# Conformer convolution on eight cores: convolution in four pieces between the next chunk's projections, last chunk in two token halves, normalised block and y written over spent u

## The chip, the cores and the metric

The kernel runs on the eight cores of one Trainium2 chip, two sequences per core and no traffic between the cores. The time is the device time of the slowest core, in microseconds (us). Executions fall into two states. In the slow state one die (cores 0 to 3 or 4 to 7) runs long at a lowered clock and the time is longer. All times here are of fast executions unless said otherwise.

Also in a "fast" execution a pair of neighbouring cores can run at clock 0.81. The clock record of the trace gives it as 0.8125, 13/16. I call such a pair *hit*.

## The reference, cut to what matters

The model has two layers (the first a gated linear recurrence, the second the convolution), each between SwiGLU feed-forward parts and followed by cross-attention. Only the convolution part changes. Per core it occurs twice, once for each sequence, at about 2040 to 2340 us and at about 4835 to 5135 us. I call these the two stages. T is 2048 tokens, D is 1024 channels (8 chunks of 128).

```python
def conformer_conv_mixer(h, w_in, b_in, dw, dw_b, ln_g, ln_b, w_out, b_out):
    a, gate = jnp.split(h @ w_in + b_in, 2, axis=-1)
    u = a * jax.nn.sigmoid(gate)                         # GLU, (B,S,D)
    u = lax.conv_general_dilated(u, dw..., padding=[(CONV_WIDTH - 1, 0)],
                                 feature_group_count=D) + dw_b     # depthwise, 31 taps, causal
    u = jax.nn.silu(layer_norm(u, ln_g, ln_b))           # LayerNorm over all 1024 channels
    return u @ w_out + b_out
```

The LayerNorm needs sums over all channels, so no token can be normalised before the convolution of its last channel chunk is done.

## The kernel before

A kernel-side list scheduler orders the instructions. The program adds operations with their reads, writes, assumed duration `d` and, for TensorE, the PSUM bank. The scheduler simulates the engines with these durations and fixes one instruction order per engine at build time.

The scheduler divides PSUM into eight banks (`NBANK = 8`). One chunk's convolution holds banks 0 to 3, the LayerNorm sums `bs` and `bq` hold two, and two are left for the projections while a convolution is held.

```python
def glu(c):                                   # projections of chunk c, 4 blocks of 512 tokens
    for blk in range(NB):
        bg = P.bank(); ba = P.bank()
        ...  # 2 x 8 matmuls 128x512 (line 948), sigmoid on ScalarE (L951),
        ...  # (a + b) * gate on VectorE (L952), 32x32 transposes into uP (L954)

def conv(c):                                  # depthwise convolution of chunk c
    b = P.bank(n=4)
    for hf in range(2):
        expand(...)                           # VectorE copies the taps into 128x128 form (L929)
        for jj in range(16):
            j = hf * 16 + jj
            for w in range(2):                # L973: N = 64 columns, read 32 elements (64 bytes) apart
                P.op("pe", ... rhs=up.ap[:, (1 - w) * 32 + j : ... : 32], ..., d=62)
    ...  # transposes out of PSUM into u2 (VectorE, L981/L987)
    ...  # per 512 tokens: copy and square (ScalarE, L991/L992), two sum matmuls (L994)

do_glu(0)
for c in range(1, KC):
    do_glu(c)
    if c - 1 < NW:                            # NW = 5
        conv(c - 1)
for c in range(min(NW, KC - 1), KC):
    conv(c)                                   # chunks 5, 6, 7: after all projections
...  # LayerNorm: mean, variance, Ln, Exp for all tokens (L1015-L1019)

def outp(blk):                                # one block of 512 tokens
    ...                                       # mean and rstd to 128 rows (L1027), rstd copied (L1028)
    for c in range(KC):
        n = nrm[c % 3]                        # three shared f32 buffers
        ...  # n = u2 + bias - mean (VectorE, L1032); n *= rstd (POOL, L1034)
        ...  # y = silu(n) (ScalarE, L1035)
    ...  # 64 output matmuls (L1042), sums added to h
```

The softmax here doesn't subtract the row's maximum and nothing guards it: scores larger than these inputs give would overflow.

## Time and profile before

| | before |
|---|---|
| time, median of fast runs | about 5739 us (5738.61, 5739.36, 5740.08; a slow run took 6629.12) |
| TensorE busy | 97% |
| first stage, core 1: first projection to first output matmul | 216.0 us |
| output part, first to last output matmul's end | 81.1 us |
| mean granted clock of an unhit core | 0.978 |

The list of cores gives the span and the mean granted clock of each. Cores 4 and 5 were hit in this execution (they ended 35 us later; their clock is 0.81 from about 3006 to 3166 us, in the second sequence's first part, which the change does not touch), the others not:

```profile
core 1: 5738.2 us, clock 0.977
core 4: 5771.1 us, clock 0.971
```

TensorE's timeline of core 4 in the steady part. The columns are start, duration, engine, line, operation, tiles, shapes and count. A bracket gives the idle time before and what ended it:

```profile
2074.91 7.24 PE L973 MATMUL ps<-arena 128*128 128x64 bf16 x64
2081.98 5.94 PE L948 MATMUL ps<-arena 128*128 128x512 bf16 x16
2087.85 0.60 PE L994 MATMUL ps<-arena,ones 128*32 128x512 bf16 x2
2088.39 1.90 PE L948 MATMUL ps<-arena 128*128 128x512 bf16 x8
```

Sixty-four convolution matmuls take 7.24 us, 113 ns each (about 110 without the tail of the last one, in the steady period). The 16 projections behind them take 5.94 us, where eight take 1.90 us a little later. The stretches of one microsecond show why (columns: window, length, TensorE busy and instructions, granted clock, share of DMA, GB/s):

```profile
2079.00:2080.00 1.00, 1.00 (x12) 0.93 1.07 217
2080.00:2081.00 1.00, 1.00 (x12) 0.50 0.96 193
2087.00:2088.00 1.00, 1.00 (x6) 1.00 0.17 29
```

The clock falls to 0.50 inside the convolution burst although TensorE is busy all the time, and is back at 1.00 at 2086.7 us, 4.7 us after the projections have resumed. The tail of the stage, same columns as the timeline above:

```profile
2211.85 7.24 PE L973 MATMUL ps<-arena 128*128 128x64 bf16 x64 [1.07 <-DVE arena L952]
...
2246.50 4.87 PE L994 MATMUL ps<-arena,ones 128*32 128x512 bf16 x8 [2.23 <-ACT arena L991]
...
2260.34 1.87 PE L1042 MATMUL ps<-arena 128*128 128x512 bf16 x4 [3.47 <-ACT arena L1035]
```

The last sum ends at 2251.4 us, the first output matmul starts at 2260.3 us. From 2216 to 2264 us the granted clock is 0.50.

### The profile page before, as it was taken

The page shows a single profiled execution, that of the slowest core. Times are in us where ns is not written, and L with a number is a line of the kernel's source. Part 1 is how long each engine was busy: PE and PEld are TensorE (multiplying, and loading weights), DVE is VectorE, ACT ScalarE, POOL GpSimd, SP SyncE. Part 2 cuts the span into 40 slices and gives each one's busy share as a digit, 9 for nine tenths or more (in the row PEclk, how much of TensorE's full clock was granted, in tenths as well). Part 3 has the DMA queues.
Part 4 walks back from the last instruction along what each step waited for, and adds up shares of the span by engine and source line. Part 5 has one row for each costly group of instructions (what it writes and reads, how often), then busy time and mean ns, then how long its engine had stood idle before and what let it go on. Part 6 is the DMA issues. An engine that isn't in the chain of part 4 may idle for free.

```text
span 5771.1 us, 89461 instructions; the slowest of 8 cores (5730.3 to 5771.1 us)
## 1 busy us (share of the span) xinstructions
PE 5594.7 (97%) x29808; PEld 2713.5 (47%) x29808; DVE 3522.3 (61%) x5299; ACT 1808.7 (31%) x2862; POOL 977.7 (17%) x1373
## 2 busy tenths in 40 slices
PE   7999999999999998999979999999999999989998
PEld 3444565444444454444434446644444444544443
DVE  5445767555765665555565566666656566565656
ACT  3323777311211134511130128762112112263112
POOL 2000444100100043200020014431001002241001
PEclk9999999999999998999988999999999999889999
DMA  6554122222222022121251212112222220221221
GB/s 148 108 106 103 30 37 45 42 37 41 37 37 41 15 41 55 34 48 34 45 146 33 35 32 33 32 38 55 35 43 37 41 37 8 48 59 23 37 41 63
DMA packets 84217, 283.14 MB, mean 49 GB/s; under 512 B 9408, under 2 KB 9408, under 8 KB 81216
## 3 DMA queue, kind: packets, MB, share of 16 engines
q0 software_dynamic: 59328, 197.16, 20.3%
q1 hardware_dynamic: 24448, 80.26, 4.1%
q8 instruction: 257, 4.21, 0.3%
q14 instruction: 184, 1.51, 0.1%
HBM read 440.96 MB, written 33.55 MB: 82 GB/s over the span
## 4 chain that ended last, share of the span: by engine, by line
PE 92%; DVE 2%; issue 2%; POOL 1%; ACT 1%; DMA 0%; DVEq 0%; SPq 0%; POOLq 0%; ACTq 0%
PE ps L638 42%; PE ps L654 21%; PE ps L1089 5%; PE ps L948 4%; PE ps L834 4%; PE ps L812 4%; PE ps L973 2%; PE ps L546 2%; PE ps L1161 2%; PE ps L1101 1%; PE ps L1042 1%; PE ps L732 1%; DVE hn_tok L542 1%; PE ps L994 1%; DVE h L658 1%
## 5 line engine op out<-in xcount | busy, mean ns | idle before, releaser
L638 PE MATMUL ps<-arena 128*128 128x512 bf16 x11264 | 2525.9, 382 | 4.1 <-DVE arena L552 3.1
L658 DVE SCALAR_TENSOR_TENSOR h<-ps,h 128x512 f32<-128x512 f32 x2816 | 1732.6, 681 | 41.0 <-PE ps L654 33.5
L638 PEld LDWEIGHTS ps<-arena 128*128 128x128 bf16 x11264 | 1106.7, 98 | 1345.1 <-issue 79.6
L641 DVE TENSOR_TENSOR arena<-ps,arena 128x512 bf16<-128x512 f32 x704 | 486.0, 691 | 1462.6 <-PE ps L638 1426.4
L640 ACT ACTIVATE arena<-ps 128x512 bf16<-128x512 f32 x704 | 420.3, 597 | 2842.6 <-PE ps L638 2832.5
L654 PE MATMUL ps<-arena 128*128 128x512 bf16 x5632 | 1301.4, 381 | 6.2 <-DVE arena L641 3.2
L654 PEld LDWEIGHTS ps<-arena 128*128 128x128 bf16 x5632 | 547.4, 98 | 682.0 <-issue 67.6
L574 POOL DMA_DIRECT2D arena<-ffn_w_in x176 | 96.0, 545 | 1834.4 <-PE ps L638 1651.9
L517 ACT ACTIVATE junk<-h 128x1024 bf16<-128x1024 f32 x288 | 303.5, 1054 | 263.3 <-DVE h L577 148.8
L542 DVE SCALAR_TENSOR_TENSOR hn_tok<-h,stat,gB 128x1024 bf16<-128x1024 f32 x256 | 332.8, 1307 | 64.8 <-POOL stat L521 25.9
L1089 PE MATMUL ps<-arena 128*128 128x512 bf16 x1536 | 363.0, 384 | 3.5 <-DVE arena L1123 2.6
L577 DVE TENSOR_TENSOR h<-ps,h 128x512 f32<-128x512 f32 x320 | 214.7, 686 | 112.4 <-PE ps L834 57.2
L520 POOL TENSOR_SCALAR stat<-stat 128x1 f32<-128x1 f32 x290 | 87.6, 302 | 995.9 <-ACT junk L517 980.7
L546 PE MATMUL ps<-ident,hn_tok 128*128 128x128 bf16 x2048 | 159.3, 228 | 95.7 <-DVE hn_tok L542 67.1
L948 PE MATMUL ps<-arena 128*128 128x512 bf16 x1024 | 246.4, 399 | 0.0
L521 POOL TENSOR_TENSOR stat<-stat,mhalf 128x1 f32<-128x1 f32 x290 | 232.9, 803 | 43.3 <-POOL stat L520 7.8
L812 PE MATMUL ps<-arena 128*128 128x512 bf16 x1024 | 234.9, 382 | 2.3 <-DVE arena L1134 2.3
L834 PE MATMUL ps<-arena 128*128 128x512 bf16 x1024 | 228.2, 379 | 0.0
L1089 PEld LDWEIGHTS ps<-arena 128*128 128x128 bf16 x1536 | 145.6, 99 | 159.5 <-issue 11.7
L546 PEld LDWEIGHTS ps<-ident,hn_tok 128*128 128x128 bf16 x2048 | 136.7, 102 | 148.8 <-issue 111.2
L574 POOL DMA_DIRECT2D arena<-ffn_w_out x88 | 48.0, 546 | 906.8 <-PE ps L654 905.8
L550 ACT ACTIVATE arena<-ps 128x1024 bf16<-128x1024 bf16 x128 | 130.5, 1021 | 132.8 <-PE ps L546 132.5
(121 smaller groups left out, 4097.9 us busy)
## 6 DMA issues: line engine op xcount, KB each, us to landing
arena<-ffn_w_in POOLq DMA_DIRECT2D x176, 512.0 KB, 6.8
arena<-ffn_w_out POOLq DMA_DIRECT2D x88, 512.0 KB, 6.2
h<-x SPq DMA_DIRECT2D x32, 512.0 KB, 7.3
arena<-hgrn_w_in POOLq DMA_DIRECT2D x64, 256.0 KB, 5.5
y<-arena SPq DMA_DIRECT2D x32, 512.0 KB, 3.3
arena<-xattn_wkv POOLq DMA_DIRECT2D x8, 1024.0 KB, 8.6
xattn_m<-arena SPq DMA_DIRECT2D x32, 256.0 KB, 3.1
xattn_v<-arena SPq DMA_DIRECT2D x16, 512.0 KB, 2.9
```

The lines of the kernel that those rows point to most:

```text
L517: P.op("act", lambda e: e.activation(out=junk[:], in_=src_tile_ap, func=AF.Square, accum_out=stat[:, 0, col:col + 1]), reads=rkeys, writes ...
L542: P.op("dve", lambda e, tt=tt, s=s: e.scalar_tensor_tensor(out=hn_tok[:, s, :], in0=h[:, tt, :], scalar=stat[:, 2, tt:tt + 1], in1=gB[:, g ...
L546: P.op("pe", lambda e, c=c, s=s, b=b: e.transpose(out=psb16(b)[:, c * 128:(c + 1) * 128], in_=hn_tok[:, s, c * 128:(c + 1) * 128], identit ...
L638: P.op("pe", lambda e, bb=bb, ga=ga, k=k, j=j: e.matmul(psb(bb), lhsT=wiv[:, ga, k, j * 128:(j + 1) * 128], rhs=hnT[:, k, blk * 512:(blk + ...
L640: P.op("act", lambda e, bg=bg, j=j: e.activation(out=sg[j].ap, in_=psb(bg), func=AF.Silu), reads=psk(bg), writes=sg[j].keys(), tbl=SILU)
L641: P.op("dve", lambda e, bu=bu, j=j: e.tensor_tensor(out=actv[:, j, :], in0=psb(bu), in1=sg[j].ap, op=ALU.mult), reads=psk(bu) + sg[j].keys ...
L654: P.op("pe", lambda e, bo=bo, j=j, t4=t4, half=half: e.matmul(psb(bo), lhsT=actv[:, j, t4 * 128:(t4 + 1) * 128], rhs=wov[:, j, half * 512: ...
L658: P.op("dve", lambda e, bo=bo, tt=tt, half=half: e.scalar_tensor_tensor(out=h[:, tt, half * 512:(half + 1) * 512], in0=psb(bo), scalar=0.5 ...
L812: P.op("pe", lambda e, b=b, k=k, mt=mt: e.matmul(psb(b), lhsT=mv[:, k, mt * 128:(mt + 1) * 128], rhs=hnT[:, k, blk * 512:(blk + 1) * 512], ...
L834: P.op("pe", lambda e, b=b, p=p, hh=hh, mt=mt, t4=t4, o=o: e.matmul(psb(b), lhsT=p.ap[:, mt * 512 + t4 * 128:mt * 512 + (t4 + 1) * 128], r ...
L948: P.op("pe", lambda e, bb=bb, a=a, k=k, blk=blk: e.matmul(psb(bb), lhsT=v[:, a, k, :], rhs=hnT[:, k, blk * 512:(blk + 1) * 512], start=(k ...
L1089: P.op("pe", lambda e, bb=bb, a=a, k=k: e.matmul(psb(bb), lhsT=v[:, a, k, :], rhs=hnT[:, k, blk * 512:(blk + 1) * 512], start=(k == 0), st ...
```

## The change

The intent has three parts.

1. *Interleave.* The convolution of chunk c-1 is cut into four pieces of 16 matmuls, one behind each block of 16 projections of chunk c, so that dense matmuls are never far apart.
2. *Halves.* The last chunk has no projections left to hide behind. It runs in two token halves (N = 32), each with its own sums and LayerNorm chain, so that the first half's chain overlaps the second half's convolution.
3. *In place.* u of seven chunks stays in SBUF, the normalisation works in place on u, and y is written over the u of the chunk before, which is spent. No shared buffers remain.

```diff
-            NW = 5
+            NH = 2 if NB >= 2 else 1
+            NW = KC - 1
...
-            nrm = [at(CP, 512, F32), at(CP + 2048, 512, F32), at(US, 512, F32)]
+            def ybuf(c, blk):
+                return y0[blk % 2] if c == 0 else at(u2[c - 1].off + blk * 2048, 512, BF16)
...
-            do_glu(0)
-            for c in range(1, KC):
-                do_glu(c)
-                if c - 1 < NW:
-                    conv(c - 1)
-            ...
+            for c in range(1, KC):
+                b = P.bank(n=4)
+                last = c == KC - 1
+                for blk in range(NB if not last else BH):
+                    glu(c, blk)
+                    for q in range(4 * blk // (BH if last else NB), 4 * (blk + 1) // (BH if last else NB)):
+                        piece(c - 1, q, b, 0, NBK)
+                out_of_psum(c - 1, b, 0, NBK)
+                for blk in range(NB):
+                    stats(c - 1, blk)
+            c = KC - 1
+            nb = NBK // NH
+            for hf in range(NH):
+                b = P.bank(n=2)
+                for q in range(4):
+                    if hf == 0 and NH > 1 and q < NB - BH:
+                        glu(c, BH + q)
+                    piece(c, q, b, hf * nb, nb)
+                out_of_psum(c, b, hf * nb, nb)
+                for blk in range(hf * BH, (hf + 1) * BH):
+                    stats(c, blk)
+                ln(hf)
...
                 for c in range(KC):
-                    n = nrm[c % 3]
-                    P.op("dve", ... out=pair(n.ap), in0=u2v(c, blk), ...)
+                    n = u2v(c, blk)
+                    y = ybuf(c, blk)
+                    P.op("dve", ... out=n, in0=n, ...)
```

The cuts ("...") leave out buffer addresses, the half-size `expand`, the split of the output weights into four loads, and the scheduler's two-bank allocation. Lines after the change: projection L975, sigmoid L978, multiply L979, transposes into uP L981, taps L955, convolution L998, transposes out of PSUM L1009/L1014, copy and square L1019/L1020, sums L1022, broadcasts L1080, rstd copy L1081, normalisation L1086 (VectorE) and L1088 (POOL), silu L1089, output L1098.

## The prediction

> **What bounds it now.** TensorE: page, PE 97% busy; chain of waits 92% PE. Only the two convolution stages change. TensorE's timeline: the first from 2044 us (first projection) to 2341 us, the second from 4874 us.
>
> First projection to first output-projection matmul (2260 us): 216 us. PE's work there, at the timeline's full-clock durations: 512 projections x 0.216 = 110.6, 512 conv matmuls x 0.1106 = 56.6, 64 sums x 0.27 = 17.3, transposes and LayerNorm broadcast 5: about 190 us. The 26 us excess:
>
> 1. Clock, steady chunks. Windows show the granted clock falling to 0.50 some 3 to 5 us after each 7.1 us conv burst begins, for 3.4 or 6.8 us. Conv matmuls keep 110 ns at either clock; the next 16 projections take 4.6 to 5.9 us, not 3.46: 7 us per stage. [...] drops at 2079.9, 2103.9, 2127.7 us lie multiples of 3.41 apart.
> 2. Clock, tail. From 2216 to 2264 us (conv of chunks 5 to 7, no projections left) it stays 0.50; sums take 0.58 instead of 0.27 us: 7 us.
> 3. PE's waits in the tail: sums, LayerNorm, first y: 11 us.
>
> **What the change does.**
> - Pieces of 16 conv matmuls (1.77 us) after 16 projections (3.46 us): every window holds at least 1.6 us of full-rate matmuls, so the clock should hold. A window with 0.7 us of projections (2148.1 to 2151.5) caused no drop; one with 0.3 did. Part 1 goes; conv of chunks 5 and 6 moves there, with most of part 2.
> - Chunk 7 stays bare, in halves of N=32. If the strided moving read (64 B apart) sets 110 ns, it halves: no extra PE work. If weight load, 7 us more per stage. I favour the read, since transposes load 128 columns every 56 ns[...].
> - The first half's LayerNorm chain (conv end to first output matmul: 16 us now) overlaps the second half's conv and sums, 6 to 9 us; 5 to 7 us stay idle.
> - y over spent u: output blocks prepare without three-buffer waits: 1 to 3 us. Block 0 stays paced at 1.23 us per chunk, later blocks by VectorE (18 us each).
> - Costs: conv and sums hold six banks, leaving two for projections; each has 3.5 to 5 us turnaround against 1 to 2 needed: 0 to 3 us. Expand copies halve in size, double in number.
>
> First output matmul comes near 198 us instead of 216 after the first projection: 18 us, plus 2 in the output part: 40 us over both stages, all on PE's path; 0.7%.
>
> **Prediction:** 5699 us, range 5680 to 5720. Faster by over 2%: 0.01; within 2%: 0.98; slower: 0.01.
>
> **Right if:** clock 1.0 from 2061 to about 2220 us; chunk period 23.1 us instead of 24.0 to 25.1; conv N=32 near 56 to 60 ns; first output matmul 16 to 20 us earlier; low clock only near chunk 7; mean clock about 0.985, not 0.978.
>
> **Wrong if:** two projection banks stall PE; N=32 conv stays at 110 ns (gain 26 us); interleaved windows still drop the clock; second LayerNorm and table loads delay block 0's silu; VectorE gives back the early start.

Two passages that did not come from this case's traces are cut from the recorded text. No term of its sum is among them: 18 us plus 2 per stage, 40 us over both stages, 5739 to 5699 us. A "window" in it is a step of 3.41 us: in the trace of the kernel before (core 4, clock record) every stretch of one clock between 2042 and 2285 us lasts 3.413 us or a multiple of it.

## More of the kernel before

Program order is priority. The order is part of the program, so an assumed duration that is wrong does not change it at run time (a convolution matmul is assumed at `d=62` ns and takes 110 in the trace).

One group of instructions, whole execution, core 4 (columns: count, busy time, mean ns of one, idle time before with its releasers):

```profile
L1032 DVE SCALAR_TENSOR_TENSOR arena<-arena,vecs,ps 128x512 f32<-128x512 f32 x64 | 46.7, 742 | 20.7 <-ACT arena L1035 9.8 <-POOL arena L1034 9.6 <-PE ps L1027 1.3
```

VectorE's subtraction of the mean waits 19.4 us for ScalarE and POOL to free one of the three shared buffers.

## The result, and the profile after

| | before | after |
|---|---|---|
| fast runs, us | 5738.61, 5739.36, 5740.08 | 5743.15, 5743.54, 5745.80 |
| ratio of fast runs | | 1.0008 (0.9986 to 1.0031): the same |
| unhit span, us (profiled execution) | about 5735 | about 5721 |
| mean clock, unhit core | 0.978 | 0.983 to 0.984 |
| pairs hit in these timed runs | none (the profiled execution: one) | 2, 2, 1 |
| first projection to first output matmul (first stage, cores 1 / 4) | 216.0 us | 216.8 us |
| output part (same cores) | 81.1 us | 64.9 us |

Ratios here and below are the mean time of one kernel's fast runs over that of the other's of the same rounds, so they are not quite the ratios of the medians that I quote. Predicted were 5699 us: the time stayed within 2%, as the prediction said, but the gain of 40 us did not come. Medians were 5744.67 us after (with its slow run of 5853.51) and 5739.72 us before.

Two things are hidden in "the same". First, the typical core did gain 14 us. Second, the slowest core hid it, as the list of cores after shows:

```profile
core 0: 5744.1 us, clock 0.979
core 1: 5743.9 us, clock 0.979
core 4: 5721.9 us, clock 0.984
```

Cores 0 and 1 ended 22 us later than the others with the same program. In TensorE's stretches they separate at one place: up to 2202 us core 0 has clock 1.00, after that 0.81 until about 2363 us (0.50 in the tail of the stage). First core 0, then core 4 (columns as before):

```profile
2195.60:2202.20 6.60, 6.60 (x32) 1.00 0.30 41
2203.00:2206.00 3.00, 3.00 (x13) 0.81 0.02 5
2270.00:2340.00 70.00, 70.00 (x315) 0.81 0.23 53
```

```profile
2203.00:2206.00 3.00, 3.00 (x18) 1.00 0.00 0
2270.00:2340.00 70.00, 68.30 (x403) 1.00 0.43 106
```

But an unhit core, too, is 22 us above the prediction, and its first output matmul comes no sooner. TensorE's timeline of core 4, an unhit one, shows what became of the interleave:

```profile
2109.00 1.93 PE L998 MATMUL ps<-arena 128*128 128x64 bf16 x16
2110.99 3.40 PE L975 MATMUL ps<-arena 128*128 128x512 bf16 x15
2114.32 0.61 PE L1022 MATMUL ps<-arena,ones 128*32 128x512 bf16 x2
2114.86 1.93 PE L998 MATMUL ps<-arena 128*128 128x64 bf16 x16
2116.71 0.60 PE L1022 MATMUL ps<-arena,ones 128*32 128x512 bf16 x2
2117.25 1.93 PE L998 MATMUL ps<-arena 128*128 128x64 bf16 x16
...
2119.64 1.93 PE L998 MATMUL ps<-arena 128*128 128x64 bf16 x16
2121.50 1.03 PE L1022 MATMUL ps<-arena,ones 128*32 128x512 bf16 x2
2122.87 11.23 PE L975 MATMUL ps<-arena 128*128 128x512 bf16 x47 [0.33 <-issue]
2133.94 1.93 PE L998 MATMUL ps<-arena 128*128 128x64 bf16 x16
```

The program says "16 projections, one piece" four times. The engine's order is 16 projections, then three pieces with the sums between them, then 48 projections in one run (one record is missing), then the fourth piece. From 2114.3 to 2122.9 us there is no projection, only pieces and eight sums. The clock falls to 0.50 there as before: it averages 0.73 from 2119 to 2124 us.

The reason stands in ScalarE's timeline of the same core, and in VectorE's:

```profile
2111.98 0.72 ACT L1019 ACTIVATE arena<-arena,vecs 128x512 bf16<-128x512 f32 x1 [3.70 <-DVE arena L1009]
...
2117.94 0.71 ACT L1020 ACTIVATE arena<-arena,vecs 128x512 bf16<-128x512 f32 x1
2118.55 0.67 ACT L978 ACTIVATE arena<-ps,vecs 128x512 bf16<-128x512 f32 x1
```

```profile
2121.75 2.71 DVE L955 COPY arena<-arena 32x512 bf16<-32x512 bf16 x1 [0.94 <-PE ps L998]
2124.38 0.73 DVE L979 SCALAR_TENSOR_TENSOR arena<-ps,vecs,arena 128x512 bf16<-128x512 f32 x1
```

The block of projections ends at 2114.4 us. Its sigmoid stands on ScalarE behind all eight copies and squares of the chunk before (four of the eight were still to come), and runs at 2118.55 us. The multiply that frees the second bank stands on VectorE behind the taps and runs at 2124.4 us. So the turnaround of the projection banks is 10.7 us (2114.4 to 2125.1). The program puts all sums of chunk c-1 ahead of the projections of chunk c+1, and program order is priority.

The part "in place" did what it should. The same group as before, core 4, and the convolution's two shapes:

```profile
L1086 DVE SCALAR_TENSOR_TENSOR arena<-arena,vecs,ps 128x512 f32<-128x512 f32 x64 | 44.8, 739 | 2.0 <-PE ps L1080 1.9
L998 PE MATMUL ps<-arena 128*128 128x64 bf16 x896 | 107.7, 287 | 6.9 <-DVE arena L955 6.9
L998 PE MATMUL ps<-arena 128*128 128x32 bf16 x256 | 16.6, 233 | 5.3 <-DVE arena L955 5.2
```

VectorE's waits before this instruction fall from 20.7 to 2.0 us. Busy time over count gives 120 ns for N = 64 and 65 ns for N = 32 in these groups. (The mean ns column shows the length of one instruction, which overlaps its neighbours.) Read from a run of 32 in the timeline, N = 32 takes 1.99 us, 62 ns each.

The tail after, core 4:

```profile
2237.19 1.99 PE L998 MATMUL ps<-arena 128*128 128x32 bf16 x32 [1.56 <-DVE arena L955]
2240.11 1.07 PE L998 MATMUL ps<-arena 128*128 128x32 bf16 x16 [0.93 <-DVE arena L955]
...
2258.75 5.52 PE L1098 MATMUL ps<-arena 128*128 128x512 bf16 x19 [1.16 <-DVE arena L1032]
```

Each half has 64 convolution matmuls, so the first half ends with the run at 2237.19, at 2239.2 us; the x16 at 2240.11 belongs to the second half. The first output matmul starts 19.6 us after the first half's end, where the undivided chain before took 16.

Where did TensorE's time go between the first projection and the first output matmul? The table counts each matmul of the first stage from its start to the next start, and gaps of more than 0.05 us as idle, on cores whose trace has all records. (c_stats_late and d_conv_whole are explained below.)

| us | before, core 3 | after, core 3 | c_stats_late, core 4 | d_conv_whole, core 4 |
|---|---|---|---|---|
| 512 projections | 120.7 | 117.3 | 114.9 | 124.3 |
| convolution | 57.2 | 59.1 | 59.4 | 58.0 |
| 64 sums | 20.1 | 20.9 | 17.9 | 14.8 |
| broadcasts and transposes | 6.6 | 10.4 | 10.8 | 10.8 |
| idle | 11.4 | 9.2 | 6.4 | 4.1 |
| sum | 216.0 | 216.9 | 209.4 | 212.0 |
| mean granted clock | 0.83 | 0.89 | 0.93 | 0.89 |

The change gained 3.4 us of projections and 2.2 us of idle time. It paid 3.8 us for the broadcasts, which the halves issue in smaller groups, and 2.7 us for convolution and sums. That is why the first output matmul came no sooner.

### The profile page after: what moved, and what is told of

It is laid out like the page before. It is cut to its first block, busy times and chain, and to the rows that moved or that the text cites. A ratio compares the mean times of both kernels' runs of the same rounds, so it can differ in the third digit from the quotient of the medians.

```text
span 5744.1 us, 90302 instructions; the slowest of 8 cores (5718.3 to 5744.1 us)
## 1 busy us (share of the span) xinstructions
PE 5586.8 (97%) x29936; PEld 2710.0 (47%) x29936; DVE 3560.3 (62%) x5467; ACT 1813.1 (32%) x2868; POOL 1001.2 (17%) x1405
## 4 chain that ended last, share of the span: by engine, by line
PE 92%; DVE 3%; issue 2%; ACT 1%; POOL 1%; DMA 0%; DVEq 0%; SPq 0%; POOLq 0%; ACTq 0%
PE ps L642 42%; PE ps L658 21%; PE ps L1145 5%; PE ps L975 4%; PE ps L838 4%; PE ps L816 4%; PE ps L1098 2%; PE ps L550 2%; PE ps L998 2%; PE ps L1217 2%; PE ps L1157 1%; PE ps L736 1%; PE ps L1022 1%; DVE h L662 1%; DVE hn_tok L546 0%
## 5 line engine op out<-in xcount | busy, mean ns | idle before, releaser
L975 PE MATMUL ps<-arena 128*128 128x512 bf16 x1024 | 245.2, 398 | 1.4 <-DVE arena L979 1.4
```

Of the source, the lines that this page charges most:

```text
L975: P.op("pe", lambda e, bb=bb, a=a, k=k: e.matmul(psb(bb), lhsT=v[:, a, k, :], rhs=hnT[:, k, blk * 512:(blk + 1) * 512], start=(k == 0), st ...
```

## The experiments

My theory after the comparison had two parts. (A) The interleave was spoiled by *order*: sums ahead of the sigmoid. If the sums are emitted late, two projection banks are enough. (B) The hits of pairs come with the bunched order, a quiet stretch of convolution followed by a long dense burst. The rivals were: two banks are too few in themselves; the hits are the chip's chance and fall on any kernel; the pieces themselves, or the denser stage, provoke them.

Sixteen runs were made in four batches, each batch on one chip, some of them with a kernel that had run before. All results were correct. In each entry "unhit" is the unhit span in us, "hits" the number of hit pairs in each fast execution. A hit is recognised by the span and mean clock of a pair of cores. Where it lies in time is known only for the executions with a trace.

### Batch 1: is it order, and is it the chip?

**b_again** is the kernel before, again, in five rounds.

> The kernel before, unchanged, to learn how often a pair of cores falls to 13/16 of the clock (0.81) for about 155 us. Theory P (that clock comes at random, to either kernel): in 5 executions about as many pairs are hit as in the changed kernel. Theory Q (the change provokes it): 0 or 1 pair hit here, against 1 to 2 pairs in every execution of the changed kernel. Unhit cores 5730 to 5738 us, hit ones some 20 to 35 us longer; time 5739 us when none is hit.

Measured: 5738.67 median of fast runs; ratio 1.0000 (0.9985 to 1.0015); unhit 5734.9. In 12 fast executions on this chip (its own five and the seven it is compared with) no pair was hit.

**a_again** is the changed kernel, again.

> The changed kernel, unchanged. Unhit cores again 5718 to 5724 us, 14 us under those of before; hit pairs near 5742 us. Theory Q: nearly every execution has a hit pair, and the time is 5742 to 5746 us. Theory P: some executions have none and take about 5725 us, ratio 0.9975.

Measured: fast 5760.34, 5743.13 and 5760.76; hits 2, 1, 2; ratio 1.0028 (1.0011 to 1.0044); unhit 5720.2. The hits repeat in another session. In its trace cores 4 to 7 are hit in both stages (5758 us) and cores 0 to 3 not (5717 to 5724 us). One hit costs about 20 us, two about 38. Core 4's onset in the first stage, seen as before in TensorE's stretches:

```profile
2170.00:2176.00 6.00, 6.00 (x29) 1.00 0.31 44
2180.00:2188.00 8.00, 8.00 (x44) 0.81 0.40 66
```

In the traces of this kernel (the profile after and a_again) the hits lie in the two convolution stages. The five onsets that were read against the timeline come 6.6 to 8.6 us into a run of 48 projections (for one, core 0 after: 2202.8 us, in the run that begins at 2195.6; core 5 of a_again: 4915.4 us, in the run that begins at 4906.8).

**c_stats_late** emits the sums of chunk c-2 one block behind each piece of chunk c-1, so that only one copy and one square stand ahead of a sigmoid. Nothing else changes, and the banks are as few as before.

```diff
-                for blk in range(NB if not last else BH):
+                nblk = NB if not last else BH
+                for blk in range(nblk):
                     glu(c, blk)
                     for q in range(...):
                         piece(c - 1, q, b, 0, NBK)
+                    if c > 1:
+                        for sb in range(NB * blk // nblk, NB * (blk + 1) // nblk):
+                            stats(c - 2, sb)
                 out_of_psum(c - 1, b, 0, NBK)
-                for blk in range(NB):
-                    stats(c - 1, blk)
...
                     piece(c, q, b, hf * nb, nb)
+                    if hf == 0 and NB > 1:
+                        for sb in range(NB * q // 4, NB * (q + 1) // 4):
+                            stats(c - 1, sb)
```

> The sums of chunk c are emitted one chunk later, one block after each piece, so that ScalarE's static order no longer puts 8 sum activations (5.6 us) ahead of the sigmoid that frees a projection bank; banks are as many as in the changed kernel. Theory A (that order bunches the pieces and so drops the clock): steady chunks take 23.1 us instead of 23.4 to 24.9, no drop of the clock between 2061 and 2220 us, and the first output matmul comes 8 to 14 us sooner per stage: unhit cores 5695 to 5708 us. Rival B (two projection banks are too few whatever the order): chunks stay at 24 us or more, with waits of the projections, and unhit cores stay near 5720 us.

Measured: fast 5714.31, 5713.99 and 5711.29; hits none; ratio 0.9955 (0.9939 to 0.9972), which is clear of 1, though under 2%; unhit 5708.9. TensorE's timeline of core 4 now has the order that the program asks for:

```profile
2126.25 1.93 PE L998 MATMUL ps<-arena 128*128 128x64 bf16 x16
2128.10 0.60 PE L1022 MATMUL ps<-arena,ones 128*32 128x512 bf16 x2
2128.64 3.63 PE L975 MATMUL ps<-arena 128*128 128x512 bf16 x16
2132.11 1.93 PE L998 MATMUL ps<-arena 128*128 128x64 bf16 x16
```

The block repeats every 5.86 us, so a chunk takes 23.44 us (predicted 23.1). TensorE's stretch of the steady part, core 4, first in this kernel and then in the changed one:

```profile
2080.00:2230.00 150.00, 147.91 (x882) 0.99 0.32 51
```

```profile
2080.00:2230.00 150.00, 144.53 (x806) 0.93 0.32 50
```

Two banks suffice when the order is right. The rival "two banks are too few" falls. The span and the chunk stay just short of what theory A expected (5695 to 5708 us, 23.1 us).

**d_conv_whole** is the changed kernel with the four pieces together behind the four blocks of projections. The interleave alone is undone in the program, and the sums stand as in the changed kernel.

```diff
                 for blk in range(NB if not last else BH):
                     glu(c, blk)
-                    for q in range(...):
-                        piece(c - 1, q, b, 0, NBK)
+                for q in range(4):
+                    piece(c - 1, q, b, 0, NBK)
```

> The four pieces of a chunk's conv stand together again behind its four projections; the rest of the change stays. Theory A: pieces were bunched in the changed kernel anyway, so this costs little: unhit cores 5718 to 5730 us. If the pieces as they stood had brought the gain of 14 us, this loses it: unhit cores 5732 us or more.

Measured: fast 5715.00, 5716.37 and 5716.01; hits none; ratio 0.9960 (0.9943 to 0.9976); unhit 5711.2. That is faster than either theory expected (5718 to 5730, or 5732 and more). This result weighs against the premise of the change. Without any piece between projections, the kernel is within 2 us of the working interleave. Its mean clock is 0.983 and that of c_stats_late 0.986, yet their spans are nearly equal. In the steady part (core 6) the granted clock is as low as in the changed kernel:

```profile
2080.00:2230.00 150.00, 148.42 (x862) 0.92 0.32 50
```

In its timeline (two bursts of 32 convolution matmuls with eight projections between) the chunk mostly repeats every 24.0 us (one per stage takes 22.6) against 23.44. Worked out from the full-clock durations that the prediction lists, a chunk needs about 23.1 us (an estimate).

Are the clock drops cheap, then? On the convolution they cost nothing: 32 of its matmuls take 3.70 us here and also in the tail of the kernel before, at clock 0.50. But the projections behind the bursts pay: 124.3 us per stage against 114.9 in c_stats_late (table above). The kernel wins 3.1 of these 9.4 us back on the sums, 1.4 on the convolution and 2.3 by idling less. So it shows that another order can do as well as the interleave; it is no clean measure of what the clock costs.

### Batch 2: what are halves and in-place work worth?

**h_bunched** is c_stats_late with the changed kernel's bunched order written down on purpose: pieces 0 to 2 and the sums behind the first block, piece 3 behind the last (the expectation says before the last; the code puts it behind). The last chunk's branch is left out here.

```diff
-                    for q in range(...):
-                        piece(c - 1, q, b, 0, NBK)
-                    if c > 1: ...
+                    elif blk == 0:
+                        for q in range(3):
+                            if c > 1:
+                                stats(c - 2, q)
+                            piece(c - 1, q, b, 0, NBK)
+                        if c > 1:
+                            stats(c - 2, 3)
+                    elif blk == 3:
+                        piece(c - 1, 3, b, 0, NBK)
```

> The kernel with the late sums, but its pieces 0 to 2 emitted together between the first and the second projection block of a chunk, with the late sums between them, and piece 3 before the last block: TensorE's order becomes nearly that of the changed kernel, for another reason (emission, not banks). Theory A2 (the bunched order itself costs the clock and provokes the 13/16 clock of core pairs): clock drops to 0.50 come back in the chunks, unhit cores rise from 5709 to 5716 to 5724 us, and core pairs are hit in most executions. Rival (only the bank waits and ScalarE's queue cost it; the order does not matter): unhit cores stay at 5708 to 5712 us. If there are no hits with the drops back, the bunched order does not provoke the 13/16 clock by itself.

Measured: fast 5732.92, 5733.71 and 5733.66; hits none here; ratio 0.9973 (0.9949 to 0.9997); unhit 5728.0. On this chip the kernel before is itself a little slower (unhit about 5739), so only kernels of this batch are compared. First output matmul 216.8 and 217.5 us after the first projection: the bunched order alone reproduces the changed kernel's front. It was not hit on this chip, so the batch does not confirm part (B).

**e_one_piece_tail** is c_stats_late with the last chunk undivided.

```diff
-            NH = 2 if NB >= 2 else 1
+            NH = 1
...
-                b = P.bank(n=2)
+                b = P.bank(n=4)
```

> On the late-sums kernel, the last chunk is undivided again, with one LayerNorm chain. The prediction counted the halves as the overlap of the first half's chain (6 to 9 us per stage). If that is right, the first output matmul comes 6 us or more later after the last projection than the 25.0 us of the late-sums kernel, and cores take 5720 us or more. If the halves bring nothing (small waits for expand copies and double the LayerNorm work eat them): 5706 to 5713 us.

Measured: two fast runs, 5721.72 and 5725.48; ratio 0.9956 (0.9932 to 0.9980); unhit 5717.1. The halves are worth a few us at most; batch 4 measures it on one chip.

**f_three_buf** is c_stats_late with the normalised block in three shared buffers again.

```diff
+            nrm = [at(CP, 512, F32), at(CP + 2048, 512, F32), at(EX + 2048, 512, F32)]
...
-                    n = u2v(c, blk)
+                    n0 = u2v(c, blk)
+                    n = pair(nrm[c % 3].ap)
```

> On the late-sums kernel, the normalised block goes through three shared buffers again instead of over its u in place; y still lies over spent u. The output part gained about 7 us per stage against the prediction's 1 to 3. If working in place did that, the blocks lose their lead: output part 4 us or more longer per stage, cores 5717 us or more. If it came from elsewhere (the clock, the early first LayerNorm): within 3 us of 5709.

Measured: fast 5747.97, 5779.31 and 5750.95; hits 0, 2, 0; ratio 1.0018 (0.9978 to 1.0058); unhit 5743.6. The gain is gone. The group of the normalisation, first in this kernel (core 1), then in c_stats_late (core 4):

```profile
L1093 DVE SCALAR_TENSOR_TENSOR arena<-arena,vecs,ps 128x512 f32<-128x512 f32 x64 | 46.9, 740 | 16.4 <-ACT arena L1096 14.4 <-PE ps L1086 1.9
```

```profile
L1091 DVE SCALAR_TENSOR_TENSOR arena<-arena,vecs,ps 128x512 f32<-128x512 f32 x64 | 44.8, 738 | 2.0 <-PE ps L1085 1.9
```

With three buffers VectorE waits for silu to free one, 14.4 us over both stages. The output part lasts 81.5 us with three buffers and 65 in place.

**g_prep_early** is c_stats_late with the first output block normalised before the second half's sums: the sums' copies wait for the rstd copy.

```diff
+                if hf > 0:
+                    late = (prep(0),)
                 for blk in range(hf * BH, (hf + 1) * BH):
-                    stats(c, blk)
+                    stats(c, blk, late if hf > 0 else ())
```

> A try to do better: on the late-sums kernel, block 0 is prepared before the second half's sums, whose ScalarE work is made to wait for the copy of block 0's 1/std. That copy stands behind four sum activations (2.9 us) now. Expected: the first output matmul comes 2 to 4 us sooner after the last projection than 25.0 us, cores 5702 to 5706 us, no core pair hit. If the sums or the table loads then delay the output matmuls as much: no change from 5709 us.

Measured: fast 5730.30 to 5733.00 in four runs; hits none; ratio 0.9969 (0.9952 to 0.9987); unhit 5725.0. This failed as an improvement. The first output matmul comes 25.7 and 25.9 us after the last projection, in c_stats_late 25.2 and 25.3. The waits only moved: TensorE's order still put sums and broadcasts first. The output part grew, too: 70.5 to 73.7 us on the profiled cores, with 4.9 us of idle time, against 65 to 67 us and at most 2.4 in c_stats_late.

### Batch 3: do the hits follow the order?

**a_third**, **h_again** and **c_again** are the changed kernel, the bunched one and the one with late sums, on a third chip.

> The changed kernel beside three variants on one chip, to settle the 13/16 clock. So far it was hit in each of 6 fast executions, every time 7 to 8 us into a burst of 48 projection matmuls (10.4 us) that follows three conv pieces and eight sums. Expected: hit pairs again in most fast executions, unhit cores 14 us under before.

> The bunched order by emission (bursts of 40 projections instead of 48). On another chip it had no hit in 3 fast executions. If the chip made that difference, it is hit here as often as the changed kernel; if the order's details do (40 against 48, sums apart), it has none beside a changed kernel that has some.

> The late-sums kernel as the reference of this chip: no hit, unhit cores 24 to 28 us under before, 10 to 14 us under the changed kernel's unhit cores.

| kernel | fast runs, us | hits | unhit | ratio |
|---|---|---|---|---|
| a_third | 5761.63, 5726.63, 5744.55, 5764.01, 5742.41 | 3, 0, 1, 1, 1 | 5721.2 | 0.9982 (0.9905 to 1.0059) |
| h_again | 5751.05, 5761.90 | 2, 2 | 5726.6 | 1.0003 (0.9884 to 1.0122) |
| c_again | 5714.02, 5712.73 | 0, 0 | 5708.6 | 0.9928 (0.9811 to 1.0046) |
| before, same rounds | 5737.26, 5803.71, 5738.15, 5739.90 | 0, 2, 0, 0 | 5734.9 | |

The bunched order costs 18 us on an unhit core (h_again against c_again). Here it is hit in both fast executions, and the interleaved one in neither of its two. The one execution of the changed kernel without a hit took 5726.63 us.

**k_bias_first** was to test whether the POOL work that runs through all chunks (bias adds) matters. It moves all 16 adds into the first chunk.

```diff
-                for tt in range((c - 1) * NT // (KC - 1), c * NT // (KC - 1)):
-                    bout_add(tt)
+                if c == 1:
+                    for tt in range(NT):
+                        bout_add(tt)
```

> The changed kernel with all of POOL's 16 output-bias adds (2.36 us each) moved to the first chunk, so that in the bursts of the later chunks POOL is idle; TensorE's order stays bunched. If POOL's work on top of the dense burst provokes the 13/16 clock, hits vanish (0 in the fast executions); if the TensorE and ScalarE order alone does, hits stay as frequent as in the changed kernel.

Measured: fast 5801.50, 5762.82 and 5764.86; hits 1, 0, 0; ratio 1.0038 (0.9939 to 1.0136); unhit 5758.4. Its stages are 37 us longer on an unhit core (the first output matmul comes 230 to 235 us after the first projection, on unhit cores of the changed kernel 213 to 218), so it says nothing about hits. It is inconclusive. It does show how far a single move of low-priority work can shift a static order.

### Batch 4: two by two on one chip

What remained open was the sum: which part of the change pays how much. All four kernels have the late sums, so the interleave works. They differ in halves and in the normalised block (in place or in three buffers); y lies over spent u in all four. **m_interleave_alone** is f_three_buf with `NH = 1` and `b = P.bank(n=4)` (the edit of e_one_piece_tail); the other three are kernels from above.

> Late sums and interleaved pieces alone: the last chunk undivided, three shared buffers. The prediction gave the interleaving about 7 us of clock and most of 7 us of tail clock per stage, 26 us or so in all. If interleaving alone brings that: unhit cores 5710 us beside 5735 of before. If it brings only what the front of the stage showed (first output matmul 3 to 6 us sooner per stage) and the lost filler eats it: 5728 to 5740 us.

> Interleaving and work in place, no halves, now beside its neighbours on one chip. Halves worth 2 us per stage by runs on different chips: unhit cores 4 us above the late-sums kernel. If the halves bring the predicted 6 us or more per stage: 12 us above or more.

> Interleaving and halves, three shared buffers. By runs on different chips the buffers cost 25 to 30 us over both stages: unhit cores 5735 to 5740 us beside 5709 of the late-sums kernel. If the chip made that, 5712 to 5716 us (the predicted 1 to 3 us per stage).

> The late-sums kernel with all three parts, the reference of these four: unhit cores 5706 to 5712 us, no hits.

| unhit span, us (before: 5734.4) | three buffers | in place |
|---|---|---|
| last chunk whole | m: 5740.9 | e: 5715.1 |
| last chunk in halves | f: 5740.7 | c: 5708.8 |

| ratio and fast runs | |
|---|---|
| m_interleave_alone | 1.0009 (0.9942 to 1.0077): 5790.70, 5824.32, 5746.37, 5791.98, 5784.16 |
| f_same_chip | 1.0021 (0.9955 to 1.0087): 5802.15, 5787.37, 5793.19 |
| e_same_chip | 0.9945 (0.9861 to 1.0029): 5749.79, 5747.77, 5752.77 |
| c_same_chip | 0.9936 (0.9856 to 1.0015): 5758.18, 5761.87, 5714.27 |
| before | 5738.35, 5770.80, 5770.58, 5769.98, 5771.31 |

In place is worth 26 us (m to e) to 32 us (f to c) over both stages. The halves are worth nothing with three buffers and 6 us in place. What is left of the change (before to m: the interleave, but also y over spent u, u of seven chunks in SBUF, and smaller tap and weight loads) costs 6.5 us; no run splits it further.

The timelines tell where the interleave's gain went. Counted on one core each, first stage, between the first and the end of the last output matmul:

| | output part, us | cross-attention projections in it | TensorE idle in it, us |
|---|---|---|---|
| before, core 1 | 81.1 | 48 | 5.7 |
| m_interleave_alone, core 5 | 81.8 | 32 | 8.2 |
| e_one_piece_tail, core 5 | 64.5 | 0 | 1.8 |
| c_stats_late, core 4 | 65.3 | 8 | 1.2 |
| after, core 4 | 64.9 | 7 | 1.2 |

Kernel m reaches its first output matmul on this core 4.9 us (first stage) and 2.4 us (second) sooner than before, but its output part is as long and does 16 fewer of the next part's matmuls as filler (3.5 us at 0.216 us each, an estimate). Together with the longer idle time this gives most of the gain back. The rest of the 6.5 us I did not follow: core 5 has the shortest span of this execution (5735.5 us), and on other unhit cores the first output matmul of the first stage comes 211.2 to 214.6 us after the first projection. Likewise the 16 us that the output part of the changed kernel is shorter contain about 9 us of filler (41 matmuls at 0.216 us, the same estimate) that only moved to later.

This chip also set a limit to part (B). Here the kernel before itself was hit in four of five fast executions, m in four of five, e and f in all three each and c_stats_late, against expectation, in two of three. In the trace of c_same_chip cores 0 to 3 were at 0.81 from about 2992 to 3160 us, where the kernel before was hit in its profile (a part that the change leaves alone), and cores 2 and 3 again in the second convolution stage, in spite of the interleaved order. TensorE's stretch there, core 2 and then core 4:

```profile
4910.00:4980.00 70.00, 68.90 (x346) 0.81 0.32 52
```

```profile
4910.00:4980.00 70.00, 69.04 (x401) 1.00 0.33 47
```

So the interleaved order can be hit, too (f_three_buf, also interleaved, had been in one of three fast executions of batch 2). Where the changed kernel ran (its first measurement, batches 1 and 3), it was hit in 10 of 11 timed fast executions (16 pairs), the kernel before in 1 of 19, c_stats_late in none of 5 and d_conv_whole in none of 3. That association is strong in these sessions. That the bunched order makes it is supported by h_again (two of two) but not by h_bunched (none of three on its chip), and on the chip of batch 4 interleaved kernels were hit in 12 of 14 fast executions (in the trace of c_same_chip one of these hits lies in the second convolution stage). So theory (B) is not shown. What lowers the clock to 0.81 stays open, as does why chips differ: no run here isolates it, and the chips of the batches differ.

### The version that beats both

c_stats_late took 5711 to 5714 us in all five fast executions on two chips, where the kernel before took 5736 to 5742 in fifteen of sixteen (5803.71 in the other) and the changed kernel 5727 to 5764 in eight. On the chip of batch 4 it was ahead as well where no pair was hit (5714.27 against 5738.35).

## Why the prediction was wrong

- **"Within 2%" held, the size did not.** Predicted 5699 (5680 to 5720); measured about 5744. Of the 45 us, about 18 are the hits of pairs (5744 against 5726.63 in the execution without). The remaining 27 are below.
- **The step that failed** is "conv and sums hold six banks, leaving two for projections; each has 3.5 to 5 us turnaround against 1 to 2 needed: 0 to 3 us". The sum counted the instructions that free the banks and not the queue in front of them. The eight copies and squares stand ahead of the sigmoid, and the measured turnaround was 10.7 us. The static order therefore bunched three pieces. "Every window holds at least 1.6 us of full-rate matmuls" was then false: 2114.3 to 2122.9 us has no projection. c_stats_late, with the same banks and another order, removes it: 12 us on an unhit core over both stages, where 0 to 3 us per stage were counted.
- **First output matmul at 198 us instead of 216: failed.** Measured 216.8 on core 4. Even with the order mended it is 207 to 211. An undivided last chunk with the mended order gives 211 to 213.
- **The clock terms (7 and 7 us): the first about right, once the order is mended; the second mis-sized.** In the changed kernel the projections gained 3.4 us of the first 7, in c_stats_late 5.8 (120.7 to 114.9 us). The tail's 7 us hardly came: the sums take 20.9 us after and 17.9 in c_stats_late, 20.1 before. The tail stays at 0.50 (before from 2216 to 2264 us, after from 2237 to 2261 us, core 4); c_stats_late still has 0.52 from 2231 to 2252 us. The low clock cost the convolution nothing (3.70 us for 32 matmuls at 0.50, and the same 110 ns each at 1.00). And the interleave was not the only way to the gain: d_conv_whole, whose mean clock is 0.92 from 2080 to 2230 us against 0.98 to 0.99, is only 2 us slower.
- **Halves, "overlaps the second half's conv and sums, 6 to 9 us": mis-sized.** They were worth 0 to 3 us per stage (batch 4). The convolution waited for half-size tap copies (1.56 and 0.93 us), and the other half's copies, squares and broadcasts lie in the first half's chain, at half clock. The chain took 19.6 us after it was cut in two; before it was 16. The broadcasts in smaller groups cost TensorE 8.3 us per stage before the first output matmul, where they took 4.4.
- **"y over spent u: 1 to 3 us": mis-sized,** and the largest single error of size in the other direction. Batch 4 gives 26 to 32 us for both stages, 13 to 16 per stage. The waits were in the profile before: 19.4 us of VectorE's idle time before L1032, released by ScalarE and POOL. The prediction put 1 to 3 us on them. (Batch 4 varies the three buffers alone, not where y lies.) Here the prediction was lucky: without this gain the changed kernel would have been slower than the kernel before also on an unhit core (an estimate: 5721 plus 26 to 32 us against 5735).
- **What was right:** N = 32 takes 62 ns (predicted 56 to 60) where N = 64 takes 110, with one weight load per matmul in both, so the columns read and not the weight load set the convolution's rate; that the stride does it is not shown. The mean clock of an unhit core is 0.984 (predicted 0.985), though it did not bring the time with it. The steady chunk, where the interleave works, is 23.44 us (predicted 23.1).
- **Not foreseen:** that the slowest core is chosen from eight, and that a core's shorter span helps nothing where a pair of them is slowed (that the order raises the chance of it is not shown). The prediction treated the core's path as the time.

What the traces show of the clock and of the convolution's read; no run isolates what makes them so:

- **The clock of 0.50.** In the kernel before (core 4) the window from 2148.1 to 2151.5 us, with 0.7 us of projections and else convolution, kept the clock at 1.00; after the one from 2124.2 to 2127.7 us, with 0.3 us, it was 0.50. TensorE was busy 100% of the stretch in which it was 0.50 (2080 to 2081 us). In the changed kernel (core 4) the clock is 0.50 from 2121.3 us, within the 8.6 us without projections.
- **The clock of 0.81.** TensorE is 97% busy in the profiles before and after, and unhit cores have a mean clock of 0.978 and 0.983 to 0.984. In the profiled executions of b_again, c_stats_late, d_conv_whole and c_again no pair was hit (mean clocks 0.978 to 0.979, 0.985 to 0.986, 0.982 to 0.983 and 0.985 to 0.987). Where the 0.81 came, it came on pairs of cores (0/1 alone in the profile after, while 2 and 3 had a mean of 0.983), and ended with TensorE as busy as before (core 0 after: busy 100% from 2300 to 2423 us, 0.81 up to 2362 and 1.00 from 2363 us). Both pairs of a die were hit together in some executions (cores 0 to 3 from about 2992 us in c_same_chip). A 128x512 matmul takes 0.265 us at this clock (core 0 after, 49 output matmuls from 2269.58 to 2282.55 us) and 0.216 at 1.00. In a slow execution of h_again core 2 was at 0.81 from 2160 to 2200 us and core 0, on the same die, at 1.00.
- **The read.** The convolution reads elements 64 bytes apart. One matmul takes 110 ns with 64 columns and 62 ns with 32, about 1.5 ns per further column (an estimate from these two). No run varies the stride, so what it costs is not shown.

## What to carry to other kernels

Under a static list schedule, the turnaround of a scarce buffer was the length of the queue in front of the instruction that frees it (10.7 us), not that of the instructions (3.5 to 5 us counted): read from the other engines' timelines what stands ahead of it, and give low-urgency work (here the sums) a place in program order behind the urgent one. Waits of an engine that is not the bottleneck can still set the length of one stage: the 19.4 us that VectorE waited for shared buffers pointed to a gain of 26 to 32 us. When a variant is used to price one cause, add up the engine's time by kind of instruction: d_conv_whole looked like proof that the clock is cheap, and its projections were 9.4 us per stage dearer. Where the time is that of the slowest of several cores, look at the whole list of cores: the same program gained 14 us on most cores and lost it again on the pair that decided the time.
